# DeltaNet: the queries' SiLU reads its bias from a tile that is written after the keys' norms

## The chip, the core and the metric

The kernel runs on one core of one Trainium2 chip. The metric is the device time of one execution in microseconds (us). The core has a matrix engine (PE, TensorE), three engines for elementwise work (DVE, VectorE; ACT, ScalarE; POOL, GpSimd), and SP, which issues most DMAs. Each engine runs its own queue in order and waits for the others by semaphores. An instruction that waits holds up all that stands behind it on its engine.

## The reference, cut to what matters

A two-layer trunk over 256 latent tokens and 256 context tokens, width 1024. The first layer mixes tokens with an RG-LRU, the second with a gated DeltaNet; each layer is a SwiGLU block, the mixer, and another SwiGLU block. The change lies in the DeltaNet, in the part that makes queries, keys and values:

```python
def dn_inputs(h, w_in, conv_w, a_log, dt_bias):
    proj = h @ w_in
    qkv = jax.nn.silu(centred_conv(proj[..., :DN_QKV], conv_w))
    q = l2norm(qkv[..., :DN_QK].reshape(bsz, t, DN_HEADS, DN_DK)) * (DN_DK ** -0.5)
    k = l2norm(qkv[..., DN_QK:2 * DN_QK].reshape(bsz, t, DN_HEADS, DN_DK))
    v = qkv[..., 2 * DN_QK:].reshape(bsz, t, DN_HEADS, DN_DV).astype(F32)
    ...
```

Each of the 8 heads then needs the decays between the tokens of a chunk of 64 (`exp` of differences of a running sum), the products of its keys with each other and with its queries, and the solution of a unit triangular system in every chunk; after that a scan over the chunks carries the state.

## The kernel before, in words

All tensors lie with features on the 128 partitions and tokens along the row; every fp32 product is made of three matmuls on split operands (`mm3`, L300 to L303). The DeltaNet layer runs in the function `deltanet`, from about 1320 to 1630 us of the span. Inside it the order of work is written as generators, which `tick` advances between the matmuls of the projections; but in this part of the program nothing fixes the order on the engines, so the compiler's scheduler sets it from what each instruction reads and writes, and may move an instruction ahead of work that stands before it in the source.

The projections (tiles `f`, 24 or 48 matmuls of 128x256 each) come in the order of `SEQ`: 8 heads of keys, 8 of queries, then values (v, 48 matmuls) and gates (z, 24 matmuls) mixed. What is done with each:

- `k_head` and `k_rest` (keys, L1056 to L1121): convolution (`conv`, one ACT instruction L787 and three DVE instructions L791), SiLU (L1067), then per head: POOL makes a diagonal of decays (`spread`, L1125, tile `gd`), PE spreads it (L1077, `gr`) and multiplies keys with keys (L1082, `kk`), DVE subtracts (L1086), ACT takes Relu (L1088) and Exp (L1089) of tile `e`, DVE makes sums of squares, reciprocals, and the masked products (L1093 to L1111), POOL copies four blocks of the result into `Bc` (L1117) and ACT four into `MO` (L1121).
- `q_head` (queries): convolution into `u`, a copy into `kq` (L1145), then the generator waits until `state["normed"]`, then SiLU in place (L1150), squares (L1053), and on PE the products with the keys (L1159) and the sums of squares (L1163), both into a PSUM bank `tq`; ACT copies the sums to `ssq` (L1165) and DVE multiplies the decays by the products (L1168).
- `norms` (L1195 to L1206): after the last head of keys, DVE makes the reciprocal square roots of all keys' sums of squares (helper `rsqrt`, L313 to L324; tile `rinv`, ending at L1201) and some small copies (L1202, L1204), and sets `state["normed"]`. That flag belongs to the program that writes the instructions; it makes no instruction wait for another.
- `v_head` (values): convolution, two SiLU instructions (L1177, L1178) into `vs`, four transposes on PE (L1184, `tv`), and ACT scales them by `rinv` (L1188). `z_head`: one SiLU (L1192).
- `solve` (L1212 to L1234): two transposes on DVE (L1216) that need all of `Bc`, 31 steps of two DVE instructions (L1225, L1228), and four closing transposes (L1231, L1232). `merge` (L1240 to L1285) then joins the halves of each chunk with matmuls `pp` (L1247) and `qq` (L1266); the scan over the chunks follows it.

ACT holds one table of functions at a time; a row ACT_TABLE_LOAD with the line of the instruction behind it stands wherever the next function is not in it. Exp (L1089) and SiLU (L1150) need different ones, Relu, Copy and Square run with either. PSUM has six banks that `f`, `gr`, `kk`, `tq`, `tv`, `pp` and `qq` share.

Of the kernel before, what the change touches and what calls it, by code (L numbers as in the profile page):

```python
# [14 lines left out]
AF = mybir.ActivationFunctionType  # L15
OP = mybir.AluOpType
# [78 lines left out]
def trunk(ctx, tc, io):  # L95
    nc = tc.nc
    PE, ACT, DVE, POOL = nc.tensor, nc.scalar, nc.vector, nc.gpsimd
# [11 lines left out]
    def slot(p, dt=F32):  # L109
        return scope["s"].tile([128, 512], dt, name=nm(p), tag="s", bufs=scope["ns"])  # L110
# [26 lines left out]
    def small(p, n, bufs=2, dt=F32, tag=None):  # L137
        return scope["s"].tile([128, n], dt, name=nm(p), tag=tag or p, bufs=bufs)

    def bank(p, tag="mm", bufs=6):  # L140
        return ps.tile([128, 512], F32, name=nm(p), tag=tag, bufs=bufs)
# [193 lines left out]
    def rsqrt(y, v, n, short=False):  # L335
        run(rsqrt_steps(y, v, n, short))
# [441 lines left out]
    def pause(n):  # L778

        for _ in range(n):  # L780
            yield

    def conv(u, p, cw, vs=V2, bias=0.0):

        c = slice(HALFS[vs[0]].start, HALFS[vs[-1]].stop)
        pv, uv = (t[:, c].rearrange("p (v t) -> p v t", t=256) for t in (p, u))
        ACT.activation(u[:, c], p[:, c], AF.Identity, scale=cw(2), bias=bias)  # L787
        for j in (1, 0, 3):
            sh = j - 2
            a, b = max(0, -sh), 256 - max(0, sh)  # L790
            DVE.scalar_tensor_tensor(uv[:, :, a:b], pv[:, :, a + sh:b + sh], cw(j), uv[:, :, a:b], OP.mult, OP.add)  # L791
            if j == 0:
                yield
        yield
# [158 lines left out]
    def deltanet(norm, next_norm, sp, hp, pools, done):  # L953
        def one(name, shape, pool=sp):
            return pool.tile(shape, F32, name=name)
# [4 lines left out]
        def slot_of(i):  # L960
            return (i // 2) ^ (i % 2)
# [9 lines left out]
        y, sg, g = (one(n, [128, 64], hp) for n in ("y", "sg", "g"))  # L971
        ea = one("ea", [128, 16], hp)
        gt = one("gt", [128, 2, 64])
        ss, ssq, rinv = one("ss", [128, 4, 8]), one("ssq", [128, 2, 8]), one("rinv", [128, 4, 8])
        KQ, QK, VN, Z, KT, GD = ({} for _ in range(6))
        eye = K_["eye"][:, None, None, :]
# [7 lines left out]
        def kcol(i):  # L984
            a = 64 * (0, 3, 2, 1)[i] if i < 4 else 256 + 128 * (i - 4) + 64 * (i % 2)
            return slice(a, a + 64)

        def qcol(i):
            a = 256 + 128 * (i - 4) + 64 * (1 - i % 2)
            return slice(a, a + 64)  # L990
# [49 lines left out]
        def pair_layout(dst, f):  # L1040

            for half, r in enumerate(ROWS):
                d = dst[r].rearrange("p (d x) -> p d x", d=2)
                f(d if half == 0 else d[:, ::-1], r)
# [3 lines left out]
        def cw(t, j):  # L1048
            return C["dn_cw"][:, j * 24 + t:j * 24 + t + 1]

        def squares(dst, kq, c):

            ACT.activation(dst.rearrange("p (b c x) -> p b c x", b=2, c=2),  # L1053
                           kq[:, 256:768].rearrange("p (b c x) -> p b c x", b=2, c=4)[:, :, c], AF.Square)
# [83 lines left out]
        def q_head(hd, p):  # L1138
            u = slot("u")
            yield from conv(u, p, lambda j: cw(hd, j), (1,))  # L1140
            kq = KQ[hd]
            kv, uv = (t.rearrange("p (b z) -> p b z", b=2) for t in (kq[:, 256:768], u[:, LAT]))
            kv = kv[:, :, 64:192]
            if "normed" not in state:
                ACT.copy(kv, uv)  # L1145
                yield
                while "normed" not in state:
                    yield WAIT
                uv = kv
            ACT.activation(kv, uv, AF.Silu)  # L1150
            sq = slot("sq")
            squares(sq[:, 0:256], kq, slice(1, 3))
            yield from pause(PACE["q_lag"])
            while hd not in state:
                yield WAIT
            tb = bank("tq")
            for i in range(4, 8):
                j = slot_of(i) - 2
                PE.matmul(tb[ROWS[i % 2], 256 + j * 64:256 + j * 64 + 64], kq[:, kcol(i)], kq[:, qcol(i)],  # L1159
                          start=True, stop=True)  # L1160
            for i in range(4, 8):
                j = slot_of(i) - 2
                PE.matmul(tb[ROWS[1 - i % 2], 384 + j:385 + j], sq[:, i * 64 - 256:i * 64 - 192], ones,  # L1163
                          start=True, stop=True)
            ACT.copy(ssq[:, :, hd], tb[:, 384:386])  # L1165
            for half, r in enumerate(ROWS):
                q_ = QK[hd][r, :, :, 64 * (1 - half):64 * (1 - half) + 64]
                DVE.tensor_tensor(q_, q_, tb[r, None, 256:384].rearrange("p d (s x) -> p d s x", s=2)  # L1168
                                  .to_broadcast([64, 2, 2, 64]), OP.mult)
# [25 lines left out]
        def norms():  # L1195

            v = small("rsv", 32)
            DVE.tensor_scalar(v, ss.rearrange("p s h -> p (s h)"), EPS, None, OP.add)
            r = rinv.rearrange("p s h -> p (s h)")
            rsqrt(r, v, 32)  # L1200
            DVE.tensor_tensor(r, r, v, OP.mult)  # L1201
            DVE.tensor_tensor(bk, bk, bp, OP.mult)  # L1202
            for dst, src in ((bkc, bk), (btc, bp)):
                pair_layout(dst, lambda d, r_: DVE.tensor_copy(d, src[r_].rearrange("p (d x) -> p d x", d=2)))  # L1204
            state["normed"] = True
            yield  # L1206

# [88 lines left out]
        next(dec)  # L1296
        pipe.live += [k_head(i, P[i]) for i in range(4)]
        f = {"k": k_head, "q": q_head, "v": v_head, "z": z_head}

        def keys():  # L1300
            live = Pipe()
            for n in range(8):
                while ("k", n) not in state:
                    yield
                live.live.append(k_rest(n))
                for _ in range(PACE["key_every"]):
                    live.tick(PACE["key_steps"])
                    yield
            while live.live:
                live.tick(3)  # L1310
                yield
            yield from norms()
            for _ in solve():
                yield from pause(PACE["solve"])
            while "contexts" not in state:
                yield
            yield from merge()
# [331 lines left out]
    with tc.tile_pool(name="dns", bufs=1, reuse_waits="tile") as dns, phase(7):  # L1649
        WS.ahead(4)  # L1650
        hpool = tc.alloc_tile_pool(name="hp", bufs=1, reuse_waits="tile")
        H = [hpool.tile([128, KD, 2, 256], F32R, name=nm("H"), tag=f"H{v}", bufs=1) for v in V2]
        ks = iter(range(KD))

        def pair(_):
            k = next(ks)
            return HL(*(Parts(H[0][:, k, i], H[1][:, k, i]) for i in range(2)))
        norm.pair = pair

        pools = [hpool, None, xctx]  # L1660

        def done(i):
            pools[i].release()
            if i == 2:
                pools[1] = tc.alloc_tile_pool(name="solve", bufs=1, side="right", reuse_waits="tile")

        deltanet(norm, next_norm, dns, hpool, pools, done)
    last = Norm(0, 0, short=True)
    with eng("PADGS"), phase(44, 2, 6, 192):
        WS.ahead(4)  # L1670
        f.run(next_norm, last, ahead=0)
        r = slot("rs")
# [96 lines left out]
```

## Time and profile before

| what | value |
|---|---|
| median of 3 runs | 1840.24 us (1838.59 to 1842.27) |
| the profiled execution: its time, its span | 1840.58 us, 1838.8 us |
| PE busy, share of the span | 1767.9 us, 96% |
| DVE busy | 1311.3 us, 71% |
| ACT busy | 807.0 us, 44% |
| POOL busy | 105.6 us, 6% |
| chain that ended last, by engine | PE 79%, DVE 10%, ACT 5%, issue 4%, DMA 2% |

The profiled execution lies 0.34 us above the median of the runs. Times in the rows below are counted from the start of its span. A row of a stretch gives the busy time of each engine in it, and behind that the clock that PE was granted (1.00 is 2.4 GHz, 0.50 is 1.2 GHz). In a row in order of time, the brackets give how long the engine stood idle before it and what ended that. fp32 matmuls show twice the count of the program (x8 for four).

### The profile page before, as it was taken

How to read it: one execution, taken by the hardware profiler on the slowest of the kernel's cores; microseconds unless marked ns; L12 is line 12 of the kernel's file. 1: busy time of each engine (PE TensorE's matmuls, PEld its weight loads, DVE VectorE, ACT ScalarE, POOL GpSimd, SP SyncE). 2: the span in 40 equal slices, each digit the busy share in tenths (PEclk: the TensorE clock that was granted, in tenths of full speed). 3: DMA queues.
4: the chain of work that ended last, by engine and by line, in shares of the span. 5: the costliest groups of instructions: out<-in, count | busy, mean ns of one | idle time of the engine just before them, and what ended most of it. 6: DMA issues, size and time to landing. Idle time of an engine off the chain costs nothing.

```text
span 1838.8 us, 28624 instructions
## 1 busy us (share of the span) xinstructions
PE 1767.9 (96%) x10806; PEld 1534.4 (83%) x10806; DVE 1311.3 (71%) x2694; ACT 807.0 (44%) x1661; POOL 105.6 (6%) x146
## 2 busy tenths in 40 slices
PE   4999999999899999999999999999999989889997
PEld 3788888888778888888898888888997988689997
DVE  7877866787878767766657655555689978776565
ACT  5532222246884433233334331332478434655454
POOL 4100000000000000000000000000006330100000
PEclk9999999999999999999999999999999989989999
DMA  9354645452133666466633675654335550025653
GB/s 348 113 185 158 220 160 171 160 200 89 46 115 126 215 214 223 178 228 207 215 113 126 218 247 198 218 199 136 105 99 166 171 175 1 1 104 188 202 184 116
DMA packets 98059, 300.59 MB, mean 163 GB/s; under 512 B 10881, under 2 KB 20353, under 8 KB 97793
## 3 DMA queue, kind: packets, MB, share of 16 engines
q1 hardware_dynamic: 92160, 277.79, 44.7%
q0 software_dynamic: 5760, 20.97, 3.7%
q8 instruction: 85, 1.39, 0.3%
q14 instruction: 54, 0.43, 0.1%
HBM read 276.70 MB, written 22.02 MB: 162 GB/s over the span
## 4 chain that ended last, share of the span: by engine, by line
PE 79%; DVE 10%; ACT 5%; issue 4%; DMA 2%; POOL 0%; SPq 0%; POOLq 0%; ACTq 0%; DVEq 0%
PE gu L302 14%; PE gu L301 14%; PE gu L303 14%; PE fo L303 4%; PE fo L302 4%; PE fo L301 4%; PE tl L301 4%; PE tl L302 4%; PE tl L303 4%; DVE u L791 2%; PE p L1386 1%; PE gu L546 1%; PE gu L542 1%; PE gu L543 1%; PE p L1417 1%
## 5 line engine op out<-in xcount | busy, mean ns | idle before, releaser
L165 ACT CAST wp<-wr 128x512 fp32r<-128x512 f32 (+1 forms) x689 | 382.7, 607 | 279.8 <-DMA wr<-in_ffn_out_dram 68.1
L166 DVE TENSOR_TENSOR wp<-wr,wp 128x512 fp32r<-128x512 f32 (+1 forms) x689 | 433.5, 676 | 98.9 <-ACT wp L165 95.3
L302 PE MATMUL gu<-hl,wp 128*128 128x512 f32 (+1 forms) x1312 | 477.0, 364 | 8.0 <-DVE hl L505 8.0
L301 PE MATMUL gu<-hh,wp 128*128 128x512 f32 (+1 forms) x1312 | 476.9, 363 | 0.9 <-ACT hh L503 0.8
L303 PE MATMUL gu<-hh,wp 128*128 128x512 f32 (+1 forms) x1312 | 476.2, 363 | 0.0
L407 DVE SCALAR_TENSOR_TENSOR junk<-ar,cb 128x1024 bf16<-128x1024 f32 x224 | 273.8, 1223 | 22.6 <-DMA ar<-in_w_adaT_dram 18.8
L302 PEld LDWEIGHTS gu<-hl,wp 128*128 128x128 f32 x1312 | 247.3, 189 | 49.0 <-DVE hl L505 10.3
L301 PEld LDWEIGHTS gu<-hh,wp 128*128 128x128 f32 x1312 | 247.4, 189 | 41.2 <-ACT hh L503 1.6
L303 PEld LDWEIGHTS gu<-hh,wp 128*128 128x128 f32 x1312 | 247.5, 189 | 38.8
L657 ACT ACTIVATE sg<-gu 128x512 f32<-128x512 f32 (+1 forms) x88 | 47.9, 544 | 362.0 <-PE gu L303 352.3
L659 DVE TENSOR_TENSOR hf<-sg,gu 128x512 f32<-128x512 f32 (+1 forms) x88 | 54.5, 620 | 177.2 <-PE gu L303 130.3
L301 PE MATMUL tl<-hidh,wp 128*128 128x256 f32 (+1 forms) x418 | 139.1, 333 | 0.0
L302 PE MATMUL tl<-hidl,wp 128*128 128x256 f32 (+1 forms) x418 | 138.6, 332 | 0.0
L303 PE MATMUL tl<-hidh,wp 128*128 128x256 f32 (+1 forms) x418 | 138.6, 332 | 0.0
L301 PE MATMUL fo<-hidh,wp 128*128 128x512 f32 (+1 forms) x352 | 127.0, 361 | 0.0
L303 PE MATMUL fo<-hidh,wp 128*128 128x512 f32 (+1 forms) x352 | 127.0, 361 | 0.0
L302 PE MATMUL fo<-hidl,wp 128*128 128x512 f32 (+1 forms) x352 | 127.0, 361 | 0.0
L301 PE MATMUL f<-H,wp 128*128 128x256 f32 x320 | 93.2, 291 | 0.0
L303 PE MATMUL f<-H,wp 128*128 128x256 f32 x320 | 91.4, 286 | 1.0 <-DVE wp L166 1.0
L302 PE MATMUL f<-H,wp 128*128 128x256 f32 x320 | 91.2, 285 | 0.0
L301 PEld LDWEIGHTS tl<-hidh,wp 128*128 128x128 f32 x418 | 79.0, 189 | 7.9
L302 PEld LDWEIGHTS tl<-hidl,wp 128*128 128x128 f32 x418 | 79.0, 189 | 7.8
(322 smaller groups left out, 2794.7 us busy)
## 6 DMA issues: line engine op xcount, KB each, us to landing
wr<-in_ffn_in_dram SPq DMA_DIRECT2D x172, 512.0 KB, 4.7
ar<-in_w_adaT_dram SPq DMA_DIRECT2D x128, 512.0 KB, 3.6
wr<-in_ffn_out_dram SPq DMA_DIRECT2D x64, 512.0 KB, 4.9
kp<-wp SPq DMA_DIRECT2D x80, 256.0 KB, 7.2
wp<-kp POOLq DMA_DIRECT2D x40, 512.0 KB, 5.0
wr<-in_dn_in_dram SPq DMA_DIRECT2D x32, 512.0 KB, 3.7
wr<-in_ffn_out_dram SPq DMA_DIRECT2D x64, 192.0 KB, 3.5
wr<-in_lru_in_dram SPq DMA_DIRECT2D x16, 512.0 KB, 3.9
```

Of the source, the lines that this page charges most:

```text
L165: ACT.copy(dst.hi, src)
L166: DVE.tensor_tensor(dst.lo, src, dst.hi.bitcast(F32), OP.subtract)
L301: PE.matmul(out, w.hi, x.hi, start=start, stop=False)
L302: PE.matmul(out, w.hi, x.lo, start=False, stop=False)
L303: PE.matmul(out, w.lo, x.hi, start=False, stop=stop)
L407: DVE.scalar_tensor_tensor(junk, raw, 1.0, cb[:, v], OP.mult, OP.mult, accum_out=m[:, t % 8, v:v + 1])
L542: PE.matmul(p[:, cols], w.hi, x.hi, start=(k == 0), stop=False)
L543: PE.matmul(p[:, cols], w.lo, x.hi, start=False, stop=False)
L546: PE.matmul(p[:, cols], w(k * 128).hi, x.lo, start=False, stop=(k == KD - 1))
L657: ACT.activation(sg[:, cols], P[0][:, cols], AF.Silu)
L659: DVE.tensor_tensor(hf[:, cols], sg[:, cols], P[1][:, cols], OP.mult)
L791: DVE.scalar_tensor_tensor(uv[:, :, a:b], pv[:, :, a + sh:b + sh], cw(j), uv[:, :, a:b], OP.mult, OP.add)
```

## The change

Three lines. A new tile `zero` is allocated (one column of it is used). At the end of `norms`, behind the last instruction on `rinv`, DVE writes `zero` as 0.0 times a column of `rinv`. The SiLU of each query head takes `zero` as its bias, where it had the constant 0.0. The result is the same; each of these 8 ACT instructions now reads a tile that is written behind the keys' norms. From `zero` on the line numbers of the new kernel are 1 higher, behind `norms` 3 higher.

```diff
@@ deltanet @@
         gt = one("gt", [128, 2, 64])
+        zero = one("zero", [128, 64])[:, 0:1]
         ss, ssq, rinv = one("ss", [128, 4, 8]), one("ssq", [128, 2, 8]), one("rinv", [128, 4, 8])
@@ q_head @@
                 while "normed" not in state:
                     yield WAIT
                 uv = kv
-            ACT.activation(kv, uv, AF.Silu)
+            ACT.activation(kv, uv, AF.Silu, bias=zero)
             sq = slot("sq")
             squares(sq[:, 0:256], kq, slice(1, 3))
@@ norms @@
                 pair_layout(dst, lambda d, r_: DVE.tensor_copy(d, src[r_].rearrange("p (d x) -> p d x", d=2)))
+
+            DVE.tensor_scalar(zero, r[:, 31:32], 0.0, None, OP.mult)
             state["normed"] = True
```

The scheduler answers with a new order on ACT, DVE, PE and POOL in the DeltaNet; SP's queue stays as it was.

ACT, where the first heads of queries meet the decays of the keys (`kq` are the queries, `e` the decays). Before:

```order
L1145 COPY kq_11471<-u_12237 128x2x128
L1150 ACT_TABLE_LOAD
L1150 ACTIVATE kq_11471<-kq_11471 128x2x128
L1145 COPY kq_11474<-u_12278 128x2x128
L1088 ACTIVATE e_12312<-e_12312 128x512
L787 ACTIVATE u_12340<-f_12266,cst 128x256
L1089 ACT_TABLE_LOAD
L1089 ACTIVATE e_12312<-e_12312 128x512
```

Now, the same place:

```order
L1146 COPY kq_11472<-u_12238 128x2x128
L1146 COPY kq_11475<-u_12279 128x2x128
L787 ACTIVATE u_12341<-f_12267,cst 128x256
L1089 ACTIVATE e_12313<-e_12313 128x512
L1090 ACTIVATE e_12313<-e_12313 128x512
```

and where the queries' SiLU went, behind the first head of values (`vs`) and the last copies into `MO`:

```order
L1178 ACT_TABLE_LOAD
L1178 ACTIVATE vs_12863<-u_12842 128x4x64
L1179 ACTIVATE vs_12863<-u_12842 128x2x2x64
L1122 COPY MO_11788<-e_12807 32x4x32 x2
L1122 COPY MO_11789<-e_12807 32x4x32 x2
L1151 ACTIVATE kq_11472<-kq_11472,zero 128x2x128
L1151 ACTIVATE kq_11475<-kq_11475,zero 128x2x128
L1054 ACTIVATE sq_12916<-kq_11472 128x256
L1054 ACTIVATE sq_12919<-kq_11475 128x256
L1151 ACTIVATE kq_11478<-kq_11478,zero 128x2x128
L1151 ACTIVATE kq_11481<-kq_11481,zero 128x2x128
```

The eight SiLU left the exponentials and stand together behind them; ten loads are gone.

PE, at the first four heads of queries, which stand behind the 48 matmuls of a value head (`f_12830`, now `f_12831`) in both programs. Before:

```order
L303 MATMUL f_12830<-H_11449,wp_12558 128x256
L1159 MATMUL tq_12941<-kq_11471 64x64 x4
L1159 MATMUL tq_12953<-kq_11474 64x64 x4
L1159 MATMUL tq_12965<-kq_11477 64x64 x4
L1159 MATMUL tq_12977<-kq_11480 64x64 x4
L301 MATMUL f_12989<-H_11448,wp_12633 128x256
L302 MATMUL f_12989<-H_11448,wp_12633 128x256
```

Now:

```order
L303 MATMUL f_12831<-H_11449,wp_12559 128x256
L1160 MATMUL tq_12943<-kq_11472 64x64 x4
L1160 MATMUL tq_12955<-kq_11475 64x64
L1164 MATMUL tq_12943<-ones,sq_12916 64x1 x4
L1160 MATMUL tq_12955<-kq_11475 64x64 x3
L1164 MATMUL tq_12955<-ones,sq_12919 64x1 x4
L1160 MATMUL tq_12967<-kq_11478 64x64 x4
L1160 MATMUL tq_12979<-kq_11481 64x64
L1164 MATMUL tq_12967<-ones,sq_12922 64x1 x4
L1160 MATMUL tq_12979<-kq_11481 64x64 x3
L1164 MATMUL tq_12979<-ones,sq_12925 64x1 x4
L301 MATMUL f_12991<-H_11448,wp_12634 128x256
```

The place in PE's queue is the same; the sums of squares, which had 22 matmuls of the next projection ahead of them, now stand ahead of that projection (18 of its matmuls then come before the other four heads of queries). The four transposes `tv` of each value head keep their places among the projections, to one or two dozen matmuls.

DVE, at the end of `solve`, where the convolution of the seventh value head (`u_13587`, now `u_13589`; the heads are v0 to v7 and this is v6) stands. Before, with 7 steps of `solve` and the closing transposes still behind it:

```order
L1228 TENSOR_TENSOR Bc<-Bc,tm_13810 128x2x9x23
L791 SCALAR_TENSOR_TENSOR u_13587<-f_13503,cst,u_13587 128x2x255
L1225 TENSOR_TENSOR tm_13813<-N,Bc 128x384
L791 SCALAR_TENSOR_TENSOR u_13587<-f_13503,cst,u_13587 128x2x254
L1228 TENSOR_TENSOR Bc<-Bc,tm_13813 128x2x8x24
L791 SCALAR_TENSOR_TENSOR u_13587<-f_13503,cst,u_13587 128x2x255
L1225 TENSOR_TENSOR tm_13816<-N,Bc 128x350
```

Now, among the closing transposes:

```order
L1231 TENSOR_TENSOR Bc<-Bc,tm_13833 128x2x31
L791 SCALAR_TENSOR_TENSOR u_13589<-f_13505,cst,u_13589 128x2x255
L1234 STREAM_TRANSPOSE A_13839<-Bc 128x32x32
L791 SCALAR_TENSOR_TENSOR u_13589<-f_13505,cst,u_13589 128x2x254
L1235 STREAM_TRANSPOSE N<-Bc 128x32x32
L791 SCALAR_TENSOR_TENSOR u_13589<-f_13505,cst,u_13589 128x2x255
L1234 STREAM_TRANSPOSE N<-Bc 128x32x32
```

The third instruction of that convolution stood 15 rows ahead of the first closing transpose and now stands behind the second one.

## Rows read from the trace of the kernel before

**Rows 1.** Stretches: busy us and count by engine, PE clock, DMA share, GB/s.
```profile
core 0: us, PE busy (x) PEld busy (x) DVE busy (x) ACT busy (x) POOL busy (x), PEclk, DMA share, GB/s
1383.95:1430.97 47.02, 41.54 (x394) 35.20 (x394) 45.54 (x113) 42.00 (x83) 32.58 (x45) 0.98 0.51 159
...
1400.00:1410.00 10.00, 8.76 (x80) 6.88 (x80) 9.88 (x25) 9.83 (x20) 8.11 (x12) 1.00 0.74 221
...
1430.32:1435.32 5.00, 5.00 (x25) 4.78 (x23) 4.66 (x14) 3.73 (x11) 2.65 (x4) 0.50 0.33 107
...
1443.24:1496.35 53.11, 53.11 (x464) 52.75 (x460) 51.52 (x90) 19.48 (x55) 16.25 (x26) 1.00 0.74 230
```

**Rows 2.** ACT's groups, 1383.7 to 1426: count | busy us, mean ns | idle before.
```profile
L1150 ACT ACT_TABLE_LOAD x5 | 6.4, 1283 | 0.1
L1089 ACT ACT_TABLE_LOAD x5 | 6.4, 1283 | 0.1
...
L1150 ACT ACTIVATE kq<-kq 128x256 f32<-128x256 f32 x8 | 3.3, 417 | 0.1
```

**Rows 3.** DVE's groups, 1383.9 to 1431.
```profile
L1105 DVE TENSOR_TENSOR qk<-e,msk 64x256 f32<-64x256 f32 x16 | 8.9, 555 | 0.2
...
L1095 DVE TENSOR_SCALAR rs<-ss 128x4 f32<-128x4 f32 x8 | 2.4, 306 | 0.0
```

**Rows 4.** DVE in order of time: start, us, instruction.
```profile
1413.19 1.97 DVE L1105 TENSOR_TENSOR qk<-e,msk 64x256 f32<-64x256 f32 x2
...
1430.28 0.69 DVE L1111 TENSOR_TENSOR e<-e,bp 128x512 f32<-128x512 f32 x1
...
1435.25 1.98 DVE L1216 STREAM_TRANSPOSE N<-Bc 128x1024 f32<-128x1024 f32 x1
...
1438.68 0.18 DVE L1201 TENSOR_TENSOR rinv<-rinv,rsv 128x32 f32<-128x32 f32 x1
```

**Rows 5.** POOL in order of time.
```profile
1413.82 1.06 POOL L1125 TENSOR_TENSOR gd<-msk,gc 128x512 f32<-128x512 f32 x1
...
1431.14 2.84 POOL L1117 TENSOR_SCALAR Bc<-e 32x256 f32<-32x256 f32 x4 [1.13 <-DVE rst L320]
```

**Rows 6.** ACT in order of time.
```profile
1432.78 1.34 ACT L1053 ACTIVATE sq<-kq 128x256 f32<-128x256 f32 x4
```

**Rows 7.** PE in order of time.
```profile
1425.95 0.92 PE L1159 MATMUL tq<-kq 128*64 128x64 f32 x24
1429.70 0.69 PE L1159 MATMUL tq<-kq 128*64 128x64 f32 x8 [2.83 <-DVE u L791]
1430.32 0.58 PE L301 MATMUL f<-H,wp 128*128 128x256 f32 x1
...
1435.32 0.59 PE L1163 MATMUL tq<-ones,sq 128*64 128x1 f32 x8
...
1439.98 0.45 PE L1159 MATMUL tq<-kq 128*64 128x64 f32 x8
...
1440.55 0.38 PE L301 MATMUL f<-H,wp 128*128 128x256 f32 x1
...
1443.24 0.66 PE L1184 MATMUL tv<-ident,vs 128*128 128x128 f32 x4
...
1485.61 0.60 PE L1184 MATMUL tv<-ident,vs 128*128 128x128 f32 x4
...
1497.72 0.22 PE L1247 MATMUL pp<-Bc,MO 32*32 32x32 f32 x2 [1.11 <-DVE Bc L1232]
```

**Rows 8.** DVE's groups, 1438.8 to 1489.6.
```profile
L791 DVE SCALAR_TENSOR_TENSOR u<-f,cst,u 128x510 f32<-128x510 f32 (+1 forms) x18 | 13.4, 743 | 0.1
L1168 DVE TENSOR_TENSOR qk<-qk,tq 64x256 f32<-64x256 f32 x13 | 5.4, 419 | 0.5 <-ACT ssq L1165 0.3
```

**Rows 9.** DVE in order of time, at the end of the solution.
```profile
1489.53 2.23 DVE L1231 STREAM_TRANSPOSE A<-Bc 128x1024 f32<-128x1024 f32 x1
1491.66 2.05 DVE L1232 STREAM_TRANSPOSE N<-Bc 128x1024 f32<-128x1024 f32 x1
```

## The prediction

> **What bounds the kernel now.** PE is busy for 96% of the span, so a change pays or costs by what it does to PE's idle time and clock. I read the stretches by engine first, and in them two regions. From 1383.95 to 1430.97, where the decays of the keys are made, PE has 5.48 us of idle time (47.02 less 41.54) [rows 1]. ACT looks like the bound there: 9.83 of 10 us busy from 1400 to 1410 [rows 1], and ten table loads of 1.283 us stand in it, 12.8 us [rows 2]. But DVE in the same 10 us has 9.88, and in the whole stretch 45.54 of 47.02, ACT 42.00 [rows 1]. Both are nearly full and wait for each other; the reader should see that DVE has 1.48 us to give back and no more. From 1443.24 to 1496.35 PE is busy for 53.11 of 53.11 us, DVE for 51.52 [rows 1]. Time that PE loses ahead of that stretch can't be made up in it.
>
> Then the order of time around 1430. PE issues the products of the first three heads of queries from 1425.95, waits 2.83 us for a DVE convolution (of values, not of queries), and makes the fourth head's at 1429.70 [rows 7]. The next projection runs until 1435.32 at the clock 0.50 (1.2 GHz) [rows 1]: 22 matmuls in 5.00 us, 0.227 each, so 0.113 at 1.00 (2.4 GHz). Ahead of that stood the wait of 2.83 us. The first value transposes (`tv` of v0) start at 1443.24, those of v6 at 1485.61, and the `pp` of the merge at 1497.72, after 1.11 us of waiting for DVE's last transpose [rows 7]. So at the end of `solve` PE and DVE are level within about a us; whichever is later in the new program sets the end.
>
> **The change, part by part.** *Removed:* ten table loads, 12.8 us of ACT [rows 2]. They lie beside DVE work that fills 45.54 of 47.02 us [rows 1]. What ACT saves reaches the path only as far as DVE stood idle (1.48) or ran lengthened operations for a reason that ACT's speed takes away. Lengthened ones there are: sixteen L1105 at 0.555 against 0.419 for an instruction of that shape (L1168), 2.2 us; eight L1095 at 0.306 against about 0.17, 1.1 us [rows 3, 8]. In the longest of them, 1.97 us for two, POOL makes a diagonal (1.06 us from 1413.82) [rows 4, 5]. POOL still makes as many, so I leave these 3.3 us where they are, and keep them for the range.
>
> The Trainium skill ("ScalarE: Activation LUTs", "Table sets: the hidden batching unit") tells to batch activation calls by set, which is what the new order on ACT does, and in "What ACT_TABLE_LOAD costs" it prices a switch at 1283 ns and a drain of 1380 ns besides. The trace has the 1283 ns, and 0.1 us of idle time for five [rows 2], so no drain shows. By the page's price the ten would be worth an estimated 26.6 us of ACT; the sum here doesn't use it.
>
> *Added:* `zero`, one DVE operation on a column, at most 0.18 as the one before it [rows 4], and a bias read on eight ACT instructions: nothing in the trace prices it; it can't gain, and I take 0 to 0.1 each. The first lies in the path once.
>
> *The new wait.* All eight SiLU wait for `zero`. Call the time that it is written T0. In the trace the chain to it reads: the last L1111 ends at 1430.97 (1430.28 and 0.69) [rows 4]; POOL's four copies into `Bc`, 1431.14 to 1433.98 [rows 5]; the two L1216, which stand ahead of the rest of the norms in DVE's queue, to 1437.23 [rows 4]; and `rinv` ends at 1438.86 [rows 4]. In the new program three L1168 (0.42 each) leave the tail of that chain, but its small instructions depend on each other and still follow one another: seven of about 0.2 behind the second L1216 make 1438.7. If DVE gives back its idle 1.48, T0 is 1437.3; that is my value, since DVE's fill is the row that bears on it. If the 3.3 of lengthening goes too, it is 1434.1; if ACT's relief gives nothing, 1438.9.
>
> *Who waits.* ACT can do little behind those SiLU: the squares are queued there, then the copies of the values. PE's queue stands: the first products `tq` are at the same place behind 48 matmuls of a value head, where PE comes at about 1425.95 [rows 7], and no independent matmul is between them and their sums of squares. So PE idles from some 1425 to T0, 12 us, where it now loses 2.83.
>
> *PE's sum from T0.* SiLU and squares of the first four heads: eight ACT operations of 0.335 (1.34 for four) [rows 6] and 0.4 of latency, T0+3.1; the last head's sums of squares, +0.5. Then 18 matmuls of the projection at the low clock, 18 x 0.227 = 4.1, since a wait of 12 us is longer than the one that now leaves it at 0.50. Then four heads of products and sums, 0.57 each (1439.98 to 1440.55) [rows 7]: 2.3. Then 24 matmuls x 0.113 = 2.7: `tv` of v0 at T0+12.7. (With T0 at 1437.3 that is 1450.0 for 1443.24.) Six projection matmuls that stood ahead of v0's `tv` now follow it, 0.7. From there the work is the same: 42.4 to `tv` of v6 (1443.24 to 1485.61) [rows 7], that is T0+55.8, and 10.7 more to 1496.35 [rows 1, 7], that is T0+66.5.
>
> *A second wait, at v6.* Its convolution moved to the closing transposes of `solve`. DVE from T0 to the first of them: 50.67 (1438.86 to 1489.53) [rows 4, 9], 1.26 more for the three L1168, 1.48 less for two L791 of 0.74 [rows 8], so 50.45. Then a transpose of 2.13, an L791, a transpose of about 2, an L791 [rows 8, 9]: the convolution ends at T0+56.0, its SiLU 0.9 later, and `tv` of v6 can start at T0+57. PE is there at T0+55.8: it waits 1.2, or up to 2.5 if PE's sum is shorter by the clock recovering sooner. The end of PE's projections is then T0+57+10.7 = T0+67.7, whichever of the two is later; without this wait T0+66.5.
>
> *The end.* `solve` itself ends on DVE some 59 us behind T0, as now (`pp`, which its last transpose releases, starts at 1497.72, 58.9 behind 1438.86) [rows 4, 7], and so ahead of PE. So `pp` starts on PE's account, at 1437.3 + 67.7 = 1505.0 against 1497.72 [rows 7]: **7.3 us later**. Behind it the same merge and scan follow, and I find nothing that gives it back.
>
> The profiled execution took 1840.58 us, 0.34 above the median of the runs. 1840.58 + 7.3 = **1847.9 us**. Bounds: T0 at 1434.1 and no wait at v6 give 1500.6, +2.9, and up to 0.8 less if PE's gaps ahead of `tq` shorten PE's order behind it as well, so 1842.7; T0 at 1438.9, the wait, and the clock falling again at v6 (some 20 matmuls x 0.113 = 2.2) give 1508.8, +11.1, so 1851.7.
>
> **The rivals.** *Faster: ACT is the true pace.* DVE's operations follow ACT's `e`, and its fullness is partly waiting inside lengthened instructions; with 12.8 us of loads gone the decays end so early that T0 comes before 1430. The point from which it decides is T0 = 1497.72 - 67.7 = 1430.0; the last L1111 would have to end 8.9 us earlier, at 1422. For it: ACT's 9.83 of 10. Against: DVE's 45.54 of 47.02. At most it returns PE's 5.48 of gaps and 2.5 of low clock (22 x 0.113), so 1832.6; a typical case is 1836. By the rule on sets of the Trainium skill ("ScalarE: Activation LUTs"), named above, the new order on ACT leads to this case.
>
> *No measurable change.* This kernel's measurement tells 0.2% (3.7 us) from nothing. T0 from 1434.1 down to 1431 puts `pp` 1 to 4 us late: all of DVE's lengthening must go and v6 must not wait. About 1842.7. The other way there is that the merge absorbs the delay; against it, PE is the chain's engine and was only 1.11 us from being last at 1497.72 [rows 7].
>
> *Slower still.* The second wait, at v6, drops the clock again as 2.83 us did at 1429.70 [rows 1, 7], and DVE gains nothing: T0 1438.9, about 1851.
>
> **How the numbers follow.** Forecast, 1845 to 1850: 0.58. Slower still: 0.17. No change, within 0.2%: 0.17, most of it on the slow side. Faster: 0.08. The range takes the forecast, the slower case and the slow half of no change: 1842.0 to 1852.0, which leaves out the fast case and some 0.1 of the rest. The likeliest case's own time is the predicted one.
>
> **What would show it.** In the changed profile: no table load at L1151 and a single one ahead of the eight SiLU; PE idle 10 us or more at the first `tq` (L1160), ended by ACT's `kq`, and PE's clock at 0.50 behind it; from the last L1112 to `zero` about 7.7 us, with POOL's copies and the two L1219 in it; `tv` of v0 12 to 13 us behind `zero`; a PE wait of 1 to 3 us at v6's `tv`, ended by ACT; `solve`'s last transpose ahead of PE's last projection, so that `pp` has no wait for DVE. The forecast is wrong if the last L1112 ends before 1425 (then ACT was the pace), if PE finds work while it waits, or if `pp` starts late and the end of the DeltaNet does not.

## The result, and the profile after

The changed kernel takes 1852.16 us (median of 6 runs, 1849.76 to 1858.83), the kernel before 1842.39 us in the 6 runs beside it (1838.59 to 1845.96): a ratio of 1.0060, 95% interval 1.0043 to 1.0077, that is 8 to 14 us slower. The ratios here and below are of the fast executions alone: one of the kernel before (2218.30 us) and one of bq12 (2217.65 us), both at a granted clock of 0.75, are left out. The direction and the main wait were forecast, the size was not: 7.3 us were forecast, some 11 measured by the ratio (the medians lie 9.8 apart), and the median lies 0.16 us above the range. In the two profiled executions the span went from 1838.8 to 1848.0 us, by 9.2; that of the changed kernel (1849.76 us) is the fastest of its six.

The profile of the changed kernel by stretches (busy us and count of each engine, PE's clock, share of DMA, GB/s), the first two the same as in [rows 1]:

```profile
core 0: us, PE busy (x) PEld busy (x) DVE busy (x) ACT busy (x) POOL busy (x), PEclk, DMA share, GB/s
1383.95:1430.97 47.02, 39.39 (x354) 32.65 (x352) 46.59 (x114) 27.46 (x66) 32.26 (x46) 1.00 0.54 170
1400.00:1410.00 10.00, 8.82 (x78) 6.72 (x76) 9.88 (x26) 4.62 (x12) 7.00 (x11) 1.00 0.66 210
...
1442.59:1446.66 4.07, 4.07 (x19) 3.85 (x18) 3.00 (x7) 3.16 (x9) 0.00 (x0) 0.50 0.00 0
1449.20:1494.28 45.08, 45.08 (x396) 44.88 (x396) 43.78 (x78) 15.79 (x45) 11.56 (x22) 1.00 0.74 228
1496.75:1507.56 10.81, 10.81 (x95) 10.68 (x95) 5.36 (x5) 4.40 (x11) 5.70 (x6) 1.00 0.62 175
```

ACT's load fell from 42.00 to 27.46 us in the stretch of the decays, and from 9.83 to 4.62 in the ten us from 1400. DVE was 9.88 of 10 before and is 9.88 of 10 now. That speaks against ACT as the pace; e4_relu_b below tests it.

PE in order of time (start, us, instruction; in brackets the idle time before it and what ended it), to be held against [rows 7]:

```profile
1438.74 0.90 PE L1160 MATMUL tq<-kq 128*64 128x64 f32 x10 [13.28 <-ACT kq L1151]
...
1446.66 0.70 PE L1160 MATMUL tq<-kq 128*64 128x64 f32 x8
...
1451.96 0.60 PE L1185 MATMUL tv<-ident,vs 128*128 128x128 f32 x4
...
1496.75 0.66 PE L1185 MATMUL tv<-ident,vs 128*128 128x128 f32 x4 [2.47 <-ACT vs L1179]
...
1507.56 0.22 PE L1250 MATMUL pp<-A,MO 32*32 32x32 f32 x2
```

PE stands idle for 13.28 us at the first products of queries, then for 2.47 at the transposes of v6, and `pp` starts without a wait, on PE's own account: 9.84 us later than at 1497.72 (the row shows the `pp` on `A`; the first one on `Bc` starts 0.02 us behind it). Between the two waits PE is full (45.08 of 45.08).

DVE in order of time:

```profile
1429.88 0.68 DVE L1112 TENSOR_TENSOR e<-e,bp 128x512 f32<-128x512 f32 x1
...
1434.89 1.91 DVE L1219 STREAM_TRANSPOSE N<-Bc 128x1024 f32<-128x1024 f32 x1
...
1437.99 0.15 DVE L1207 TENSOR_SCALAR zero<-rinv 128x1 f32<-128x1 f32 x1
...
1447.93 3.50 DVE L1169 TENSOR_TENSOR qk<-qk,tq 64x256 f32<-64x256 f32 x8 [2.20 <-ACT ssq L1166]
...
1490.62 2.24 DVE L1234 STREAM_TRANSPOSE A<-Bc 128x1024 f32<-128x1024 f32 x1
...
1495.21 0.67 DVE L791 SCALAR_TENSOR_TENSOR u<-f,cst,u 128x510 f32<-128x510 f32 x1
```

`zero` ends at 1438.14. The row at 1447.93 is one that the prediction hadn't counted: DVE, in the middle of `solve`, waits 2.20 us for products of queries that PE hasn't made yet. The last row is the end of v6's convolution, behind two closing transposes.

ACT in order of time:

```profile
1429.22 1.28 ACT L1178 ACT_TABLE_LOAD   x1 [2.60 <-DVE u L791]
...
1438.18 0.91 ACT L1151 ACTIVATE kq<-kq,zero 128x256 f32<-128x256 f32 x2 [5.83 <-DVE zero L1207]
1438.99 0.71 ACT L1054 ACTIVATE sq<-kq 128x256 f32<-128x256 f32 x2
```

One table load remains at that place, and ACT, which held ten of them, now waits 5.83 us for `zero`.

### The profile page after: what moved, and what is told of

Read it like the earlier page. It is cut to its first block, busy times and chain, and to the rows that moved or that the text cites. A ratio compares the mean times of both kernels' runs of the same rounds, so it can differ in the third digit from the quotient of the medians.

```text
span 1848.0 us, 28610 instructions
## 1 busy us (share of the span) xinstructions
PE 1766.9 (96%) x10806; PEld 1533.9 (83%) x10806; DVE 1312.6 (71%) x2695; ACT 795.6 (43%) x1651; POOL 104.7 (6%) x146
## 4 chain that ended last, share of the span: by engine, by line
PE 79%; DVE 11%; ACT 4%; issue 4%; DMA 2%; SPq 0%; POOL 0%; POOLq 0%; ACTq 0%; DVEq 0%
PE gu L302 14%; PE gu L301 14%; PE gu L303 14%; PE fo L303 4%; PE fo L302 4%; PE fo L301 4%; PE tl L301 4%; PE tl L302 3%; PE tl L303 3%; DVE u L791 1%; DVE wp L166 1%; PE p L1389 1%; DMA wr<-in_ffn_in_dram 1%; PE gu L542 1%; PE p L1420 1%
## 5 line engine op out<-in xcount | busy, mean ns | idle before, releaser
L301 PE MATMUL f<-H,wp 128*128 128x256 f32 x320 | 91.8, 287 | 0.4 <-issue 0.4
L303 PE MATMUL f<-H,wp 128*128 128x256 f32 x320 | 90.0, 281 | 1.0 <-DVE wp L166 1.0
L302 PE MATMUL f<-H,wp 128*128 128x256 f32 x320 | 89.6, 280 | 0.0
```

The source lines that it names most:

```text
L301: PE.matmul(out, w.hi, x.hi, start=start, stop=False)
L302: PE.matmul(out, w.hi, x.lo, start=False, stop=False)
L303: PE.matmul(out, w.lo, x.hi, start=False, stop=stop)
```

## The experiments

Each was timed on one chip beside the kernel before; a ratio is to that kernel, with its 95% interval. The column on PE's idle time gives its longest waits at the first products of the queries (in the kernel before 2.83 us, at the fourth head; in bq12 also at the fourth, in bq4 at the fifth). The column pp is the start of the first `pp` on `Bc`, which needs the last transpose of `solve`, in the profiled execution, in us from the 1497.72 of the kernel before.

| kernel | what it is | ratio | us | PE idle at the first products | pp |
|---|---|---|---|---|---|
| changed | the change | 1.0060 (1.0043 to 1.0077) | +11 | 13.28 | +9.8 |
| e1_const | `zero` a constant | 1.0005 (0.9992 to 1.0019) | +1 | 2.97 | -0.1 |
| e4_relu_b | before, no SiLU of queries | 1.0004 (0.9988 to 1.0021) | +1 | 2.82 | -0.7 |
| e2_rsv | `zero` 7 us earlier | 1.0017 (1.0000 to 1.0034) | +3 | 7.48 | +2.3 |
| e3_ss | `zero` 10 us earlier | 1.0014 (0.9999 to 1.0030) | +3 | 2.84 and 1.04 | +2.4 |
| e6_late | `zero` 4.6 us later | 1.0087 (1.0071 to 1.0103) | +16 | 16.33 | +16.4 |
| q4 | changed, lag 4 | 1.0042 (1.0018 to 1.0066) | +8 | 7.42 | +4.5 |
| q12 | changed, lag 12 | 1.0063 (1.0042 to 1.0084) | +12 | 4.46 | +9.4 |
| bq4 | before, lag 4 | 1.0013 (1.0000 to 1.0026) | +2 | 2.33 | +0.4 |
| bq12 | before, lag 12 | 1.0009 (0.9992 to 1.0026) | +2 | 2.20 | +1.1 |
| p_a | changed, products on POOL | 1.0118 (1.0093 to 1.0142) | +22 | 13.28 | +16.6 |
| p_q12 | lag 12, products on POOL | 1.0032 (1.0018 to 1.0047) | +6 | 3.87 | +5.3 |
| p_b | before, products on POOL | 1.0013 (0.9999 to 1.0027) | +2 | 2.82 | +1.1 |

The us are the ratio times the 1840 us of the kernel before. Down the table the time goes by pp, within the intervals except for p_a, which is 0.5 us outside, while no single one of the waits sorts it.

**The bias operand: e1_const.**

```diff
         zero = one("zero", [128, 64])[:, 0:1]
+        DVE.memset(zero, 0.0)
...
-            DVE.tensor_scalar(zero, r[:, 31:32], 0.0, None, OP.mult)
             state["normed"] = True
```

> The changed kernel, but zero is a constant that DVE writes at the start of the DeltaNet, so nothing waits for the norms; the queries' SiLU still read a bias tile. The order on PE is that of the kernel before, word for word, and the ten table loads are back. My theory (the loss is the wait): -0.5 to +1.5 us against before, PE idle at the first products of queries under 4 us as before. Rival (the bias operand or the longer form of the SiLU costs): +5 us or more although nothing waits.

Its ratio can't be told from 1. PE in order of time has the wait of the kernel before back:

```profile
1429.85 0.45 PE L1161 MATMUL tq<-kq 128*64 128x64 f32 x8 [2.97 <-DVE u L791]
```

Only the dependence makes the difference; the bias operand costs nothing that shows in the time, though each SiLU takes some 0.5 us with it for 0.417 [rows 2].

**The ten table loads: e4_relu_b.**

```diff
-            ACT.activation(kv, uv, AF.Silu)
+            ACT.activation(kv, uv, AF.Relu)
```

> The kernel before with Relu in place of the queries' SiLU: left out is the sigmoid of the queries, and with it the ten table loads among the decays, without any new wait. This prices the loads by themselves. Theory (DVE is the pace there, the loads lie beside it): last L1111 at most 2 us earlier, -0.5 to -3 us against before. Rival (ACT was the pace, its relief is worth most of the 12.8 us and the wait ate it): -6 to -9 us.

DVE and PE in order of time, the last L1111 and the `pp` behind `solve`:

```profile
1429.36 0.68 DVE L1111 TENSOR_TENSOR e<-e,bp 128x512 f32<-128x512 f32 x1
```
```profile
1497.04 0.22 PE L1247 MATMUL pp<-Bc,MO 32*32 32x32 f32 x2 [1.17 <-POOL Yp L1274]
```

Without the loads the last L1111 starts 0.92 us earlier than at 1430.28 [rows 4] and `pp` 0.68 earlier; in the time nothing shows (1.0004). The rival that ACT was the pace falls: 12.8 us of its work were worth less than one.

**How early must `zero` be: e2_rsv, e3_ss, e6_late.** In e2_rsv, behind the first instruction of the norms:

```diff
             DVE.tensor_scalar(v, ss.rearrange("p s h -> p (s h)"), EPS, None, OP.add)
+            DVE.tensor_scalar(zero, v[:, 31:32], 0.0, None, OP.mult)
...
-            DVE.tensor_scalar(zero, r[:, 31:32], 0.0, None, OP.mult)
             state["normed"] = True
```

> The changed kernel, but zero is written from the sums of squares of all keys (rsv, at 1429.7 in the changed kernel's trace) instead of from their reciprocal roots (1438.1): 8.3 us earlier, same order on ACT, same place of the products on PE, ten loads still gone. Theory of the wait: PE's idle time at the first products falls from 13.3 to about 5 us, the second wait at v6 shrinks or goes, and the time comes back to -1 to +3 us against before (8 to 11 under the changed kernel). Rival (the grouping of the SiLU and the order that the scheduler made of it is what costs, on PE, DVE or at v6): +6 to +11 us against before.

In e3_ss, in `k_rest` of the last head:

```diff
             DVE.tensor_scalar(rs, ss[:, :, hd], EPS, None, OP.add)
+            if hd == 7:
+                DVE.tensor_scalar(zero, rs[:, 0:1], 0.0, None, OP.mult)
             yield
...
-            DVE.tensor_scalar(zero, r[:, 31:32], 0.0, None, OP.mult)
             state["normed"] = True
```

> The changed kernel, but zero is written from the last head's own sums of squares, one DVE instruction that stands at about 1427 in the trace: the queries' SiLU still wait for the last keys, so they stay behind all exponentials and the ten loads stay gone, but not for the norms. The first products should start at about 1429 to 1430, as the last of the first four did in the kernel before. Theory (time goes by the moment at which PE gets its first products): -1 to +2 us against before, PE idle there 3 to 4 us. Rival (an order with the SiLU behind the exponentials loses something of its own): +3 us or more.

In e6_late:

```diff
             DVE.tensor_scalar(zero, r[:, 31:32], 0.0, None, OP.mult)
+            for _ in range(9):
+                DVE.tensor_scalar(zero, zero, 0.0, None, OP.mult)
             state["normed"] = True
```

> The changed kernel with nine more instructions of the same small kind behind the first on zero, each depending on the one before, interleaved with steps of solve: the steps come no later for it than by nine small instructions, but the queries' SiLU start some 3 us later. The order on ACT is the same, on PE nearly. In DVE's queue v6's convolution moved one transpose further back, with its last instruction behind all four. Theory (PE's idle time at the first products goes one to one into the end, and a conv that stands behind a closing transpose of solve adds a second wait): PE idle 16 us at the first products, a wait of 4 us or more at v6, time +4 to +7 us against the changed kernel, +13 to +17 against before. Rival (slack elsewhere takes up later SiLU): within 2 us of the changed kernel.

PE in order of time, of e2_rsv (first two rows), e3_ss (two) and e6_late (three):

```profile
1433.35 0.90 PE L1160 MATMUL tq<-kq 128*64 128x64 f32 x10 [7.48 <-ACT kq L1151]
...
1499.97 0.22 PE L1250 MATMUL pp<-A,MO 32*32 32x32 f32 x2
```
```profile
1429.60 1.12 PE L1162 MATMUL tq<-kq 128*64 128x64 f32 x16 [2.84 <-ACT kq L1153]
1433.40 1.12 PE L1162 MATMUL tq<-kq 128*64 128x64 f32 x16 [1.04 <-ACT kq L1153]
```
```profile
1443.36 0.90 PE L1160 MATMUL tq<-kq 128*64 128x64 f32 x10 [16.33 <-ACT kq L1151]
...
1501.71 1.08 PE L1185 MATMUL tv<-ident,vs 128*128 128x128 f32 x4 [3.20 <-ACT vs L1179]
...
1514.15 0.22 PE L1252 MATMUL pp<-A,MO 32*32 32x32 f32 x2
```

From the first products to `pp` it is 66.6 us in e2_rsv, which doesn't wait at v6 (1499.97 less 1433.35), and 66.3 in the changed kernel and 67.6 in e6_late once the waits at v6 are taken off (68.82 less 2.47, 70.79 less 3.20). So the moment of the first products goes into `pp` nearly one to one. The 1.3 us that e6_late has more goes with PE's clock behind its wait at v6, as a row of that stretch shows (0.50):

```profile
1502.00:1505.00 3.00, 3.00 (x16) 3.00 (x15) 0.00 (x0) 1.15 (x4) 0.00 (x0) 0.50 0.33 120
```

e2_rsv and e6_late have the changed kernel's order on ACT and the same place of the first products, so neither the order on ACT nor the grouping of the SiLU costs by itself more than what e2_rsv has left over, 0 to 6 us. DVE's order isn't the same: in e2_rsv the closing transposes follow one another (1490.34, 1492.50, 1494.42 and 1496.42) with nothing of v6 between them, so the step from it to the changed kernel holds the later `zero` and v6's new place together.

What is left over at `pp` in e2_rsv and e3_ss is gone behind the merge. The first matmul of the scan that reads the merge's result `Yp`, in the kernel before, the changed kernel and e2_rsv:

```profile
1521.17 1.06 PE L1406 MATMUL p<-vn,Yp 128*128 128x128 f32 x8
```
```profile
1530.50 1.06 PE L1409 MATMUL p<-vn,Yp 128*128 128x128 f32 x8
```
```profile
1520.64 1.06 PE L1409 MATMUL p<-vn,Yp 128*128 128x128 f32 x8
```

The changed kernel is 9.3 us late there, e2_rsv 0.5 early, and e3_ss 0.7 late (1521.85): with `zero` 7 us earlier nothing of the loss is left in the profiled execution.

In e6_late the first products come 4.6 us later than in the changed kernel, 1.6 of it because PE reaches them later (at 1427.03 for 1425.46) and 3.05 by the longer wait. Its times came as expected, but its wait at v6 was expected at 4 us or more and is 3.20; in e2_rsv PE's idle time was expected at about 5 us and is 7.48. e3_ss, at 2.6 us, lies between the theory's +2 and the rival's +3, and its interval holds both; its gain over e2_rsv is less than can be measured.

**Giving PE work to do: q12, and its control bq12.** Both with

```diff
-    "steps": 4, "decay_steps": 1, "key_every": 4, "key_steps": 3, "solve": 4, "q_lag": 2, "v_lag": 6, "k_lag": 4,
+    "steps": 4, "decay_steps": 1, "key_every": 4, "key_steps": 3, "solve": 4, "q_lag": 12, "v_lag": 6, "k_lag": 4,
```

> The changed kernel with a lag of 12 instead of 2 steps between a query's SiLU and its products, which puts 79 more projection matmuls (79 x 0.113 = 8.9 us) ahead of the first products in PE's queue. zero is written as late as in the changed kernel. Theory (the loss is PE standing with an empty hand, not T0 itself): PE's idle time at the first products falls from 13.3 to about 4 us, and the time comes back by 6 to 9 us, to 0 to +4 us against before. Rival (a late T0 holds the values and PSUM as well, so PE stops elsewhere): still +7 us or more.

> The kernel before with the lag of 12: the control for the changed kernel with that lag, without any wait for the norms. If the lag by itself moves DVE's multiplications to a place where they wait for PE inside solve, it is slower than before too, by +3 to +8 us; if the late zero is what hurts there, it is within -3 to +2 us of before.

PE in order of time in q12:

```profile
1439.37 0.45 PE L1160 MATMUL tq<-kq 128*64 128x64 f32 x8 [4.46 <-ACT kq L1151]
...
1507.16 0.26 PE L1250 MATMUL pp<-Bc,MO 32*32 32x32 f32 x2 [4.88 <-DVE Bc L1235]
```

and DVE:

```profile
1441.82 1.73 DVE L1169 TENSOR_TENSOR qk<-qk,tq 64x256 f32<-64x256 f32 x4 [1.19 <-ACT ssq L1166]
1445.70 0.85 DVE L1169 TENSOR_TENSOR qk<-qk,tq 64x256 f32<-64x256 f32 x2 [2.15 <-ACT ssq L1166]
1448.44 0.85 DVE L1169 TENSOR_TENSOR qk<-qk,tq 64x256 f32<-64x256 f32 x2 [1.90 <-ACT ssq L1166]
...
1455.07 3.50 DVE L1169 TENSOR_TENSOR qk<-qk,tq 64x256 f32<-64x256 f32 x8 [1.22 <-ACT ssq L1166]
```

My expectation was wrong here and the rival right, in a form that I hadn't had. PE's idle time did fall to 4.46 us. But the products of the eight heads are now spread between projection matmuls at the low clock (PE's clock is 0.51 from 1440 to 1450), and the multiplications stand among the first steps of `solve` in DVE's queue: four waits, 6.5 us, and `solve` now ends last, with 4.88 us of PE waiting for its last transpose. The same lag without the late `zero` (bq12) is within measurement of the kernel before, although PE waits as long at its `pp`:

```profile
1498.82 0.26 PE L1247 MATMUL pp<-Bc,MO 32*32 32x32 f32 x2 [4.88 <-DVE Bc L1232]
```

So that wait comes with the lag; what the late `zero` adds are DVE's waits ahead of it, and with them `pp` comes 8.3 us later than in bq12. At each lag that was tried `zero` hurts: PE or DVE pays.

**A lag of 4: q4, and its control bq4.** The same line with 4.

> The changed kernel with a lag of 4 instead of 2 steps: 48 more projection matmuls (5.4 us) ahead of the first products, all eight heads' products in one group on PE and on DVE, and v6's convolution 11 steps of solve ahead of its transposes, as in the kernel before. zero as late as in the changed kernel. Theory (13.3 us of idle PE, plus the wait at v6): PE idle about 8 us, none at v6, DVE loses some 3 us to the products among the first steps of solve; time +2 to +6 us against before, 4 to 8 under the changed kernel. Rival (as with the lag of 12, what PE gains DVE loses): +8 us or more.

> The kernel before with the lag of 4: the control for q4, and a try at the 2.83 us that PE waits there for a convolution of values, since 12 more projection matmuls stand ahead of the first products. Theory: PE's wait shrinks below 2 us, the stretch of low clock may go; -4 to +1 us against before. Rival (the products come later and stop DVE among the first steps of solve): +1 to +4 us.

```profile
1440.11 0.90 PE L1160 MATMUL tq<-kq 128*64 128x64 f32 x10 [7.42 <-ACT kq L1151]
```
```profile
1437.69 0.69 PE L1159 MATMUL tq<-kq 128*64 128x64 f32 x8 [2.33 <-ACT u L787]
```

q4 (PE in order of time, first fence) does what 48 matmuls can: PE is idle for 7.42 us, v6 doesn't wait, and `pp` comes at 1502.23, 5.3 us before the changed kernel's. Its time lies between what the two theories gave, and its interval overlaps the changed kernel's, so the gain of 3 us by the ratios isn't settled. The trace says more: the scan's first `p` on `Yp` is 4.7 us late (1525.90), within what the theory gave, and the profiled execution loses another 7.6 us of its span behind the DeltaNet, where the program is the same. From 1680 to 1820 PE is never idle, in the kernel before (first row) and in q4 (second), and gets through fewer matmuls at the same granted clock:

```profile
1680.00:1820.00 140.00, 140.00 (x1238) 140.00 (x1237) 85.58 (x156) 69.83 (x144) 0.00 (x0) 1.00 0.56 185
1680.00:1820.00 140.00, 140.00 (x1191) 140.00 (x1190) 80.93 (x148) 67.11 (x138) 0.00 (x0) 1.00 0.56 181
```

So the time of that execution, and with it q4's ratio, holds something that isn't of the change. bq4 (second fence of this part) was to shorten the 2.83 us of the kernel before: it moved them to another place, and gained nothing.

**Taking DVE out: p_a, p_q12, p_b.** In each, on the changed kernel, the one with lag 12, and the kernel before:

```diff
             ACT.copy(ssq[:, :, hd], tb[:, 384:386])
+            qc = sp.tile([128, 128], F32, name=nm("qc"), tag="qc", bufs=4)
+            ACT.copy(qc, tb[:, 256:384])
...
-                DVE.tensor_tensor(q_, q_, tb[r, None, 256:384].rearrange("p d (s x) -> p d s x", s=2)
-                                  .to_broadcast([64, 2, 2, 64]), OP.mult)
+                POOL.tensor_tensor(q_, q_, qc[r, None, :].rearrange("p d (s x) -> p d s x", s=2)
+                                   .to_broadcast([64, 2, 2, 64]), OP.mult)
```

> The changed kernel, with the products of the queries copied out of PSUM by ACT and multiplied by POOL instead of DVE (L1169). DVE then has no instruction among the steps of solve that waits for PE, and 6.7 us less work; PE's idle 13 us at the first products stay. Theory (13 us of idle PE are the main loss, DVE's wait of 2.2 us for the products only adds the second wait at v6): v6's transposes don't wait, pp 2 to 3 us earlier than in the changed kernel, time +6 to +9 us against before. Rival (DVE's queue is what costs): back to -2 to +3 us.

> The kernel with the lag of 12 (79 projection matmuls ahead of the first products), and the products multiplied by POOL as in p_a. Both waits are then taken away: PE is idle for about 4.5 us at the first products, DVE can't be stopped by PE inside solve. Theory (the lag moved PE's idle time to DVE, whose multiplications stood ahead of solve's steps and waited 6.5 us): pp starts at 1499 to 1502, time 0 to +4 us against before, 7 us or more under q12. Rival (T0 delays solve or the values in another way): within 3 us of q12.

> The kernel before with the products multiplied by POOL: the control for p_a and p_q12. PE is busy from 1443 to 1496 and DVE's last transpose comes 1.1 us later, so taking 6.7 us from DVE can give at most 1.1 us: -1.5 to +1 us against before; more than +2 would say that POOL's and ACT's added work costs by itself.

p_a missed by far, to the wrong side. DVE's steps of `solve` ahead of POOL's multiplications and beside them:

```profile
1442.81 0.44 DVE L1233 TENSOR_TENSOR Bc<-Bc,tm 128x270 f32<-128x270 f32 x1
...
1444.21 0.90 DVE L1233 TENSOR_TENSOR Bc<-Bc,tm 128x312 f32<-128x312 f32 x1
```

POOL's group, and PE in order of time:

```profile
L1171 POOL TENSOR_TENSOR qk<-qk,qc 64x256 f32<-64x256 f32 x16 | 16.2, 1015 | 4.3 <-ACT qc L1168 3.4
```
```profile
1462.20 0.66 PE L1187 MATMUL tv<-ident,vs 128*128 128x128 f32 x4 [1.28 <-ACT vs L1181]
...
1496.00 1.12 PE L1187 MATMUL tv<-ident,vs 128*128 128x128 f32 x4 [4.79 <-ACT vs L1181]
```

A step of `solve` that takes some 0.5 us by itself (0.48 for 312 columns in the changed kernel) takes 0.90 while POOL multiplies. The scheduler put a convolution of values among the closing transposes once more, an earlier head's this time, for which PE waits 4.79 us at 1496.00: `solve` ends 5.3 us before the changed kernel's (1494.59 for 1499.88) and nothing comes of it. So p_a doesn't tell PE's idle time from DVE's wait, as it was meant to. What it does show is how long PE waits for a convolution behind a closing transpose.

p_q12 keeps PE's first wait at 3.87 us and recovers about half of q12's loss, as far as the intervals go (1.0018 to 1.0047 against 1.0042 to 1.0084), though expected at 0 to +4 and measured at +6. DVE was to wait for PE no more inside `solve`. It waits for no product itself, but once for the first instruction of a convolution on ACT, and that stands there behind copies that wait for PE. DVE in order of time, then ACT:

```profile
1453.69 0.75 DVE L791 SCALAR_TENSOR_TENSOR u<-f,cst,u 128x510 f32<-128x510 f32 x1 [5.96 <-ACT u L787]
```
```profile
1448.08 0.16 ACT L1166 COPY ssq<-tq 128x2 f32<-128x2 f32 x1 [2.91 <-PE tq L1164]
...
1452.99 0.67 ACT L787 ACTIVATE u<-f,cst 128x512 f32<-128x512 f32 x1
```

So the 6.5 us of DVE's waits in q12 became 5.96 by way of ACT.

p_b, the control, was expected at +1 at most and has +2 (0 to +5). PE waits 2.28 and 2.06 us at two `tv` for ACT, and `pp` is 1.1 us late; that the move costs something by itself isn't clear of noise. None of these versions beats the kernel before.

## Why the prediction came out as it did

*What bounds it; the loads.* Right. DVE was the pace, ten loads were worth under 1 us at the last L1111 and at `pp` (e4_relu_b), and the rival *faster* never came near the point from which it decides: the last L1112 ended at 1430.56, not before 1422.

*T0.* Put at 1437.3, it was 1438.14. The step said that DVE gives back 1.48 us of idle time. It gave back 1.05 (46.59 busy for 45.54), but its work grew: the operations lengthened beside POOL didn't go, they moved. DVE's groups of the changed kernel, to be held against [rows 3]:

```profile
L1106 DVE TENSOR_TENSOR qk<-e,msk 64x256 f32<-64x256 f32 x16 | 7.4, 460 | 0.2
L1112 DVE TENSOR_TENSOR e<-e,bp 128x512 f32<-128x512 f32 x8 | 6.9, 867 | 0.0
...
L1096 DVE TENSOR_SCALAR rs<-ss 128x4 f32<-128x4 f32 x8 | 3.8, 474 | 0.0
```

The first fell from 8.9 to 7.4 us; the last rose from 2.4 to 3.8, and the middle one from 5.6 (0.703 each in the kernel before) to 6.9. Of the 1.48 us there were 0.41 left at the last L1112. Each of these instructions that is clearly lengthened overlaps one of POOL's in time, though not each that overlaps one is lengthened. The longest, DVE's row and POOL's:

```profile
1414.54 1.31 DVE L1112 TENSOR_TENSOR e<-e,bp 128x512 f32<-128x512 f32 x1
```
```profile
1414.24 1.06 POOL L1126 TENSOR_TENSOR gd<-msk,gc 128x512 f32<-128x512 f32 x1
```

The Trainium skill ("SBUF — State Buffer", "Who interferes with whom") says that a DVE instruction with two SBUF inputs contends with a GpSimd instruction that reads SBUF; in p_a the steps of `solve`, which have two, nearly doubled beside such instructions, and the trace agrees. That rule doesn't cover L1096, which reads one tile and lengthened as well.

*PE's idle time.* Right: some 12 us forecast, 13.28 measured, ended by ACT's `kq`, with the clock at 0.50 behind it.

*PE's sum from T0.* `tv` of v0 at T0+13.8, for 12.7 (1451.96 less 1438.14). The 18 matmuls at the low clock took 4.07 for 4.1. The first four heads took 4.45 from T0 for 3.6 (to 1442.59): a pair of SiLU is 0.91 and a pair of squares 0.71, where I had taken 0.67 for any two from the squares alone, though [rows 2] has the SiLU at 0.417 each. From `tv` of v0 to v6 it took 0.8 less than the sum had (42.3 for 43.1), so that PE came to v6 at T0+56.1 for T0+55.8.

*The second wait, at v6.* This is the term that was mis-sized. It was there, at its place and ended by ACT, but 2.47 us long for 1.2 (2.5 stood as its upper end, for another reason). The step counted DVE from T0 to the first closing transpose at 50.45 us, taking each L1168 as 0.42 of work. It took 52.48 (1490.62 less 1438.14), and 2.20 of that is the wait in front of eight of them: products that the new order asks for between steps of `solve`, before PE, whose clock was 0.50 until about 1447, has made them. I had asked who waits behind ACT's SiLU on ACT and PE, and not on DVE. q12 shows what that wait can do when it grows. `tv` of v6 came at T0+58.6 for T0+57, and `pp` at T0+69.4 for T0+67.7.

*The end.* 0.84 of T0 and 1.7 behind it make `pp` 9.84 us late for 7.3; of the 1.7, 1.3 are the longer wait at v6, 0.3 PE's later arrival there, 0.1 what follows. The forecast put what the merge gives back at nothing. It gave 0.5 here (9.3 us late at the scan's first `p`, 9.2 at the end of the span), and 2.8 in e2_rsv.

*The range.* Its top end, 1851.7, was built on one profiled execution of 1840.58 us. The kernel before then ran at a median of 1842.39 over six runs, 1.8 above it (in the later rounds, of 21 to 25 runs, at 1839.93 to 1840.73). With the bounds of T0 and the clock, but without DVE's wait and without that drift, the range was too narrow; the drift alone is more than the 0.16 us by which it was missed.

*No measurable change.* The 1 to 4 us of its case hold the wait at v6 (1431 and 1434.1 plus 67.7), though it says that v6 must not wait; without it they are 0 to 3 us.

*Slower still.* Its mechanism, that the wait at v6 drops the clock, didn't happen in the changed kernel: from 1496.75 to 1507.56 the granted clock is 1.00. It did in e6_late, behind 3.20 us.

What stays open: by how much DVE's wait and the wait at v6 would each come down alone. No run took one of them away with everything else in place; q4 has no wait at v6, but a different order on DVE too.

## What to carry to other kernels

An engine that is 98% busy need not be the pace if another is 99% busy beside it: taking 12.8 us from the one gave under 1 us here, and the wait that bought it cost PE, which is full everywhere behind, 10 us more of idle time than the one it replaced. When a wait is added, list what is queued behind the waiting instruction on its engine, then who waits for those, and then what stands behind *these* in their queues: the third step, DVE's multiplications among the steps of `solve`, was the one missed. Where a scheduler orders the engines, moving work to fill a hole can move the wait: three attempts to fill PE's idle time (q4, q12, p_q12) each gave part of it to DVE.

## What the runs showed of the hardware that was not expected

POOL's and DVE's elementwise instructions stretch each other. Sixteen POOL instructions of 64x256 took 1.015 us each in p_a, and DVE's steps beside them went from some 0.5 to 0.90 us; six of the same POOL instructions in p_q12, while DVE stood idle, took 0.73:

```profile
L1171 POOL TENSOR_TENSOR qk<-qk,qc 64x256 f32<-64x256 f32 x6 | 4.4, 730 | 0.4
```

A wait of 2.47 us of PE at v6 was followed by the clock 1.00, while the one of 2.83 us at 1429.70 [rows 7] was followed by 0.50 [rows 1], and so was bq4's of 2.33 us at 1437.69 (0.50 from 1438 to 1441). So the length of the wait alone doesn't decide it, and the runs don't tell what does.

At one granted clock, 1.00, PE made 1238 matmuls from 1680 to 1820 us in the kernel before and 1191 in q4, never idle in either; p_b has 1191 as well, and its span grew by 6.9 us from 1645 on. The runs don't tell why.
